# Combining two experts' outputs: a tile in two VectorE instructions, engines synchronised by hand

## The chip, the cores and the metric

The kernel runs on one core of a Trainium2 chip. The metric is the device time of one execution in microseconds; the kernel before takes 241.44 us (median of three runs, 241.16 to 241.47). The engines that matter here are VectorE (DVE in the profile), ScalarE (ACT), and SyncE (SP), which issues transfers; the transfers themselves run on the core's DMA engines. Slower, same or faster is judged at 2%.

## The reference

Each of 16 x 1024 tokens has two expert outputs of 512 values and two weights. The result is their weighted sum, all in float32:

```python
batch, seq, hidden, n_experts, k = 16, 1024, 512, 8, 2
# expert_outputs: (batch, seq, k, hidden), combine_weights: (batch, seq, k)
weights = combine_weights[..., np.newaxis]
return np.sum(expert_outputs * weights, axis=2).astype(np.float32)
```

So 67 MB are read and 33.6 MB are written, for three arithmetic operations per result.

## The kernel before

The 16,384 tokens are spread over 128 partitions, 128 tokens on each, and handled in 16 tiles of 8 tokens per partition (J = 8). A tile's load is 4 MB, its store 2 MB. There are four input and four output buffers. The framework places all waits between engines.

```python
wt = wpool.tile([P, per * k], dt)
for t, c in ((0, main), (main, J)):
    nc.scalar.dma_start(            # weights: 120 KB for tiles 0-14, then 8 KB for the last
        out=wt[:, k * t : k * (t + c)].rearrange("p (t k) -> p t k", k=k), in_=cw(t, c))

for g in range(per // J):
    et = ipool.tile([P, J, k * h], dt)       # 4 buffers
    ot = opool.tile([P, J, h], dt)           # 4 buffers
    nc.sync.dma_start(out=et, in_=eo(g * J, J))
    c0 = 0
    for c in (2, 2, 2, 2) if g == last else (J,):
        for i in range(c0, c0 + c):
            # ... w0, w1: this token's two weights, one value per partition
            if t == 0 or g == last:
                nc.scalar.activation(out=ot[:, i, :], in_=et[:, i, 0:h], func=copy, scale=w0)
            else:
                nc.vector.tensor_scalar_mul(out=ot[:, i, :], in0=et[:, i, 0:h], scalar1=w0)
            nc.vector.scalar_tensor_tensor(
                out=ot[:, i, :], in0=et[:, i, h : 2 * h], scalar=w1,
                in1=ot[:, i, :], op0=mult, op1=add)
        (nc.sync if g == last else nc.scalar).dma_start(
            out=o(g * J + c0, c), in_=ot[:, c0 : c0 + c, :])
        c0 += c
```

A tile is thus 16 VectorE instructions over 512 elements per partition: eight products and eight multiply-and-adds. ScalarE makes the first product of the first token and those of the last tile.

Of the kernel before, what the change touches and what calls it, by code (L numbers as in the profile page):

```python
# [1 line left out]

# [4 lines left out]


@with_exitstack
def kernel(  # L10
    ctx: ExitStack,
    tc: tile.TileContext,
    expert_outputs: bass.AP,
    combine_weights: bass.AP,
    out: bass.AP,
):

    nc = tc.nc  # L20
    b, s, k, h = expert_outputs.shape
    assert k == 2
    n = b * s
    P = nc.NUM_PARTITIONS
    per = n // P
    assert per * P == n
    J = 8
    main = per - J
    eo = expert_outputs.rearrange("b s k h -> (b s) (k h)")
    cw = combine_weights.rearrange("b s k -> (b s) k")  # L30
    o = out.rearrange("b s h -> (b s) h")

    def rows(x):

        a = x[0 : P * main, :].rearrange("(p t) f -> p t f", p=P)
        b = x[P * main : n, :].rearrange("(p t) f -> p t f", p=P)
        return lambda t, c: a[:, t : t + c, :] if t < main else b[:, t - main : t - main + c, :]

    eo, cw, o = rows(eo), rows(cw), rows(o)

    dt = mybir.dt.float32
    mult = mybir.AluOpType.mult
    add = mybir.AluOpType.add
    copy = mybir.ActivationFunctionType.Copy

    last = per // J - 1

    wpool = ctx.enter_context(tc.tile_pool(name="w", bufs=1))
    ipool = ctx.enter_context(tc.tile_pool(name="in", bufs=4))
    opool = ctx.enter_context(tc.tile_pool(name="out", bufs=4))  # L50

    wt = wpool.tile([P, per * k], dt)
    for t, c in ((0, main), (main, J)):
        nc.scalar.dma_start(
            out=wt[:, k * t : k * (t + c)].rearrange("p (t k) -> p t k", k=k), in_=cw(t, c)
        )

    for g in range(per // J):
        et = ipool.tile([P, J, k * h], dt)
        ot = opool.tile([P, J, h], dt)  # L60
        nc.sync.dma_start(out=et, in_=eo(g * J, J))  # L61
        c0 = 0
        for c in (2, 2, 2, 2) if g == last else (J,):
            for i in range(c0, c0 + c):
                t = g * J + i
                w0, w1 = wt[:, 2 * t : 2 * t + 1], wt[:, 2 * t + 1 : 2 * t + 2]


                if t == 0 or g == last:
                    nc.scalar.activation(out=ot[:, i, :], in_=et[:, i, 0:h], func=copy, scale=w0)  # L70
                else:
                    nc.vector.tensor_scalar_mul(out=ot[:, i, :], in0=et[:, i, 0:h], scalar1=w0)  # L72
                nc.vector.scalar_tensor_tensor(  # L73
                    out=ot[:, i, :],
                    in0=et[:, i, h : 2 * h],
                    scalar=w1,
                    in1=ot[:, i, :],
                    op0=mult,
                    op1=add,
                )  # L80

            (nc.sync if g == last else nc.scalar).dma_start(  # L82
                out=o(g * J + c0, c), in_=ot[:, c0 : c0 + c, :]
            )
            c0 += c


# [1 line left out]
_INS = ['expert_outputs', 'combine_weights']  # L89
_OUTS = [((16, 1024, 512), 'float32')]  # L90


# [23 lines left out]
```

## Time and profile before

| What | Value |
|---|---|
| time, median | 241.44 us |
| span of the profiled execution | 239.5 us |
| VectorE busy | 133.3 us, 247 instructions |
| ScalarE busy | 7.0 us, 10 instructions |
| bytes moved | 100.81 MB |
| a tile's load, issue to landing (median) | 49.5 us |
| a tile's store, issue to landing (median) | 24.1 us |

The page of the profile begins with the busy time of each engine. Below it the span is cut into 40 slices of 6 us: a digit is the busy share of a slice in tenths, and the row GB/s is what the DMA engines moved. Then come the DMA queues, the chain of work that ended last, the costliest groups of instructions (source line, engine, operation, output and inputs with their shapes, count; busy time and mean ns of one; idle time before them and what ended it), and the DMA issues (size of each, median time from issue to landing). Line 61 of the kernel is the load, 82 the stores, 72 and 73 the two VectorE instructions, 70 the ScalarE product, 54 the weights.

### The profile page before, as it was taken

Reading aid. Unit: us, or ns where it says so; the run is one execution under the profiler, and the core shown is the slowest. Engines: PE = TensorE matmul, PEld = TensorE weight load, DVE = VectorE, ACT = ScalarE, POOL = GpSimd, SP = SyncE. Lnnn points to the kernel's source line nnn. Section 1 sums busy time; section 2 is a strip of 40 time slices with the busy share of each in tenths; the row PEclk is TensorE's granted clock in tenths of the full one; section 3 lists DMA queues with packets and bytes.
Section 4 is the critical chain, followed back from the end, with each engine's and each line's share of the span. In section 5 each row is a group of like instructions: output and inputs, shape, how many; then the busy total and the mean of one; then the engine's idle time right before and its main releaser. Section 6 shows DMA issues by size and latency. Waiting matters only on the chain.

```text
span 239.5 us, 382 instructions
## 1 busy us (share of the span) xinstructions
DVE 133.3 (56%) x247; ACT 7.0 (3%) x10; POOL 0.2 (0%) x4
## 2 busy tenths in 40 slices
DVE  0077928529185490945819277291852918549080
ACT  0030000000000000000000000000000000000080
POOL 0000000000000000000000000000000000000000
DMA  7999899999999999999999999999999999999995
GB/s 268 451 441 439 350 438 476 401 432 424 411 441 435 479 394 438 435 441 400 435 438 441 435 460 413 438 402 432 437 435 479 397 438 427 449 397 435 438 409 213
DMA packets 5330, 100.81 MB, mean 421 GB/s; under 512 B 720, under 2 KB 848, under 8 KB 1360
## 3 DMA queue, kind: packets, MB, share of 16 engines
q1 hardware_dynamic: 2880, 69.21, 67.6%
q10 hardware_dynamic: 2448, 31.59, 30.9%
q14 instruction: 2, 0.02, 0.0%
HBM read 67.24 MB, written 33.55 MB: 421 GB/s over the span
## 4 chain that ended last, share of the span: by engine, by line
DMA 56%; DVE 26%; another core or an unknown queue 13%; issue 1%; SPq 0%; ACT 0%; DVEq 0%; ACTq 0%
DMA et<-in_expert_outputs_dram 56%; DVE ot L73 17%; DVE ot L72 10%; SPq L61 0%; ACT ot L70 0%; DVEq L111 0%; ACTq L82 0%; DVEq L72 0%; ACTq L70 0%
## 5 line engine op out<-in xcount | busy, mean ns | idle before, releaser
L72 DVE TENSOR_SCALAR ot<-et,wt 128x512 f32<-128x512 f32 x119 | 52.3, 481 | 93.7 <-DMA et<-in_expert_outputs_dram 80.2
L73 DVE SCALAR_TENSOR_TENSOR ot<-et,wt,ot 128x512 f32<-128x512 f32 x128 | 89.8, 745 | 6.7 <-ACT ot L70 6.7
L70 ACT ACTIVATE ot<-et,wt 128x512 f32<-128x512 f32 x9 | 5.7, 709 | 212.2 <-DMA et<-in_expert_outputs_dram 212.2
L70 ACT ACT_TABLE_LOAD x1 | 1.3, 1283 | 13.4 <-DMA et<-in_expert_outputs_dram 13.4
L100 POOL MEMSET const-bfloat16-1.0<- 128x1 bf16 x1 | 0.1, 102 | 0.0
L100 POOL MEMSET const-uint8-127<- 128x1 uint8 x1 | 0.1, 102 | 0.0
L100 POOL MEMSET const-float32-0.0<- 128x1 f32 x1 | 0.1, 99 | 0.2 <-issue 0.2
L100 POOL MEMSET const-float32-1.0<- 128x1 f32 x1 | 0.1, 99 | 0.0
## 6 DMA issues: line engine op xcount, KB each, us to landing
et<-in_expert_outputs_dram SPq DMA_DIRECT2D x16, 4096.0 KB, 49.5
out_dram<-ot ACTq DMA_DIRECT2D x15, 2048.0 KB, 24.1
out_dram<-ot SPq DMA_DIRECT2D x4, 512.0 KB, 4.9
wt<-in_combine_weights_dram ACTq DMA_DIRECT2D x1, 120.0 KB, 12.8
wt<-in_combine_weights_dram ACTq DMA_DIRECT2D x1, 8.0 KB, 22.1
```

Source lines behind the costliest of these rows:

```text
L70: nc.scalar.activation(out=ot[:, i, :], in_=et[:, i, 0:h], func=copy, scale=w0)
L72: nc.vector.tensor_scalar_mul(out=ot[:, i, :], in0=et[:, i, 0:h], scalar1=w0)
L73: nc.vector.scalar_tensor_tensor(out=ot[:, i, :], in0=et[:, i, h : 2 * h], scalar=w1, in1=ot[:, i, :], op0=mult, op1=add,)
L100: nc = _bacc.Bacc("TRN2", target_bir_lowering=False, num_devices=1)
```

## The change

Two things change. A tile other than the last becomes two VectorE instructions: one product of the whole 8 x 2 x 512 elements with the weights, broadcast along the last dimension, in place in the input buffer; and one sum of the two halves into the output buffer. And the whole kernel lies in one critical section with semaphores set by hand: one for each load, one for each output buffer's stores, and counters for VectorE and ScalarE. The aim is fewer instructions and fewer waits. Where the waits stand changes too: SyncE waits for the store of tile g-4 before it issues the load of tile g, so that VectorE needs to wait for the load alone; VectorE waits once for both transfers of weights; ScalarE runs a one-element activation before it issues the weights. The last tile keeps its form.

```diff
+    loaded = [nc.alloc_semaphore(f"loaded{g}") for g in range(G)]
+    stored = [nc.alloc_semaphore(f"stored{i}") for i in range(NOUT)]
+    # ... weights, tail, vec, act
+    made = [2 * (g + 1) for g in range(G - 1)]
+    with tc.tile_critical():
+        for g in range(G):
+            if g >= NOUT:
+                nc.sync.wait_ge(stored[g % NOUT], 16 * (g // NOUT))
+            ins = nc.sync.dma_start(out=et[:, g % NIN], in_=eo(g * J, J).rearrange("p j (k h) -> p j k h", k=k))
+            if g >= NIN:
+                ins._wait_ge(vec, made[g - NIN])
+            ins.then_inc(loaded[g], 16)
+
+        nc.scalar.activation(out=warm, in_=one, func=copy)
+        for t, c in ((0, main), (main, J)):
+            nc.scalar.dma_start(out=wt[:, t : t + c], in_=cw(t, c)).then_inc(weights, 16)
+        for g in range(G - 1):
+            nc.scalar.dma_start(out=o(g * J, J), in_=ot[:, g % NOUT])._wait_ge(
+                vec, made[g]
+            ).then_inc(stored[g % NOUT], 16)
+
+        nc.vector.wait_ge(weights, 32)
+        for g in range(G - 1):
+            ek = et[:, g % NIN].rearrange("p j k h -> p (j k) h")
+            wb = wt[:, g * J : (g + 1) * J].rearrange("p j k -> p (j k)").unsqueeze(2)
+            nc.vector.tensor_tensor(
+                out=ek, in0=ek, in1=wb.to_broadcast([P, J * k, h]), op=mult
+            )._wait_ge(loaded[g], 16).then_inc(vec, 1)
+            e = et[:, g % NIN]
+            nc.vector.tensor_tensor(
+                out=ot[:, g % NOUT], in0=e[:, :, 0], in1=e[:, :, 1], op=add
+            )._wait_ge(vec, made[g] - 1).then_inc(vec, 1)
+        # ... the last tile: ScalarE's eight products, VectorE's eight multiply-and-adds,
+        # ... stores of two tokens each by SyncE; then SyncE waits for all stores
-            for i in range(c0, c0 + c):
-                # ... the pairs of instructions per token, shown above
```

More of the change, by code (lines that the diff above doesn't have):

```diff
@@ L27 @@
     J = 8
+    NIN = NOUT = 4
+    G = per // J
     main = per - J
-    eo = expert_outputs.rearrange("b s k h -> (b s) (k h)")
-    cw = combine_weights.rearrange("b s k -> (b s) k")
-    o = out.rearrange("b s h -> (b s) h")
     def rows(x):
@@ L37, in rows @@
         return lambda t, c: a[:, t : t + c, :] if t < main else b[:, t - main : t - main + c, :]
-    eo, cw, o = rows(eo), rows(cw), rows(o)
+    eo = rows(expert_outputs.rearrange("b s k h -> (b s) (k h)"))
+    cw = rows(combine_weights.rearrange("b s k -> (b s) k"))
+    o = rows(out.rearrange("b s h -> (b s) h"))
     dt = mybir.dt.float32
@@ L44 @@
     copy = mybir.ActivationFunctionType.Copy
[L46 to L63, printed above, removed]
-            for i in range(c0, c0 + c):
[L65 to L85, printed above, removed]
@@ new lines @@
+    pool = ctx.enter_context(tc.tile_pool(name="sbuf", bufs=1))
+    wt = pool.tile([P, per, k], dt)
+    warm = pool.tile([P, 1], dt)
+    et = pool.tile([P, NIN, J, k, h], dt)
+    ot = pool.tile([P, NOUT, J, h], dt)
+    loaded = [nc.alloc_semaphore(f"loaded{g}") for g in range(G)]
+    stored = [nc.alloc_semaphore(f"stored{i}") for i in range(NOUT)]
+    weights = nc.alloc_semaphore("weights")
+    tail = nc.alloc_semaphore("tail")
+    vec = nc.alloc_semaphore("vec")
+    act = nc.alloc_semaphore("act")
@@ new lines @@
+    one = nc.const_aps.tensor(1.0, (P, 1), dt)
+    PIECE = 2
+    made = [2 * (g + 1) for g in range(G - 1)]
[25 more added lines that the diff above has]
+            )._wait_ge(vec, made[g] - 1).then_inc(vec, 1)
+        g = G - 1
+        nc.scalar.wait_ge(weights, 32)
+        for i in range(J):
+            e, r = et[:, g % NIN, i], ot[:, g % NOUT, i]
+            w = wt[:, g * J + i]
+            ins = nc.scalar.activation(out=e[:, 0], in_=e[:, 0], func=copy, scale=w[:, 0:1])
+            if i == 0:
+                ins._wait_ge(loaded[g], 16)
+            ins.then_inc(act, 1)
+            nc.vector.scalar_tensor_tensor(
+                out=r, in0=e[:, 1], scalar=w[:, 1:2], in1=e[:, 0], op0=mult, op1=add
+            )._wait_ge(act, i + 1).then_inc(vec, 1)
+            if i % PIECE == PIECE - 1:
+                f = i + 1 - PIECE
+                nc.sync.dma_start(
+                    out=o(g * J + f, PIECE), in_=ot[:, g % NOUT, f : i + 1]
+                )._wait_ge(vec, made[g - 1] + i + 1).then_inc(tail, 16)
+        for i in range(NOUT):
+            nc.sync.wait_ge(stored[i], 16 * len(range(i, G - 1, NOUT)))
+        nc.sync.wait_ge(tail, 16 * (J // PIECE))
```

## The prediction, made before the change was run

> **What bounds the kernel now.** I read the page from the top. First the two sections on the span and the transfers:
>
> ```profile
> span 239.5 us, 382 instructions
> ...
> DVE 133.3 (56%) x247; ACT 7.0 (3%) x10; POOL 0.2 (0%) x4
> ...
> DMA  7999899999999999999999999999999999999995
> GB/s 268 451 441 439 350 438 476 401 432 424 411 441 435 479 394 438 435 441 400 435 438 441 435 460 413 438 402 432 437 435 479 397 438 427 449 397 435 438 409 213
> ...
> HBM read 67.24 MB, written 33.55 MB: 421 GB/s over the span
> ```
>
> VectorE (DVE) works 56% of the span; the row DMA reads 9 in almost every slice except the first and last. The kernel is a copy machine: 100.8 MB at some 430 GB/s are 234 us, and only about 5 us of head and tail are not transfer. So nothing that VectorE saves can shorten the span much; a change can only add idle DMA time, or shave the 5 us.
>
> The chain that ended last, in order of time, says the same, two stretches of it shown:
>
> ```profile
> 60.76 49.49 DMA et<-in_expert_outputs_dram
> 110.25 0.03 issue
> ...
> 118.92 49.44 DMA et<-in_expert_outputs_dram
> 168.36 0.03 issue
> ```
>
> A load issued at 60.76 lands 49.5 us later, because three older loads are queued in front of it: the load queue is never empty. From 110.25 to 168.36 four tiles pass: 58.1 / 4 = **14.5 us per tile**, the DMA's pace. Then the groups and the DMA issues:
>
> ```profile
> L72 DVE TENSOR_SCALAR ot<-et,wt 128x512 f32<-128x512 f32 x119 | 52.3, 481 | 93.7 <-DMA et<-in_expert_outputs_dram 80.2
> L73 DVE SCALAR_TENSOR_TENSOR ot<-et,wt,ot 128x512 f32<-128x512 f32 x128 | 89.8, 745 | 6.7 <-ACT ot L70 6.7
> L70 ACT ACT_TABLE_LOAD x1 | 1.3, 1283 | 13.4 <-DMA et<-in_expert_outputs_dram 13.4
> ...
> out_dram<-ot ACTq DMA_DIRECT2D x15, 2048.0 KB, 24.1
> ...
> wt<-in_combine_weights_dram ACTq DMA_DIRECT2D x1, 120.0 KB, 12.8
> wt<-in_combine_weights_dram ACTq DMA_DIRECT2D x1, 8.0 KB, 22.1
> ```
>
> VectorE idles 80 us for loads. The last line matters most for the change: the second weights transfer, 8 KB, takes **22.1 us** to land. Before, only the last tile reads it.
>
> [...]
> - [...] the first transfer lands with tile 0 (12.8 us against 12.6 for the first load) and the second with tile 1 (22.1 against 21.9).
> - [...] 481 ns for the one-tensor product and 745 ns for the two-tensor operation over 512 elements.
> - [...]
>
> **The change part by part.**
>
> *VectorE's work.* Before, a tile is 8 pairs; in the chain two products take 0.79 and two sums 1.32 us, so 4 x 2.11 = 8.5 us. After, one product over 8 x 2 x 512 = 8192 elements and one sum over 4096, both two-tensor fp32, [...] I take **13.25 us, up by 4.7 per tile**: fewer instructions, [...]. It is still under the 14.5 us of the DMA, so in the steady state all of it is hidden: cost 0. If it exceeded 14.5, the excess would count 15 times.
>
> *Weights.* VectorE now waits for both weights transfers before its first tile, and ScalarE issues them only after a warm-up activation with its table load: [...]. Two or so load packets later than before's 23.3, so the first product starts at about **25 us instead of 13.5**.
>
> *The load gate.* SP now waits before load g for the store of tile g-4 to have landed, where before it waited for VectorE only. This takes a store's time to landing out of the slack of four input buffers: loads queue two or three deep instead of four. In the steady state the loop of four tiles has 4 x 14.5 = 58 us; load 15, VectorE 13, store 20 to 24 are within that, so the load queue still never empties: cost 0.
>
> *The start, where the two meet.* Sizes: a load alone takes 21.9 - 12.6 = 9.3 to 9.8 us (with its later issue 9.8), a store of half the bytes 4.9. From the packet and landing records I read about 1.5 us between a transfer's last byte, its landing, the next issue and that one's first byte.
> - Loads 0 to 3 land at 13.3, 23.1, 32.9, 42.7 with no store between them.
> - VectorE ends tiles 0, 1, 2, 3, 4 at 25 + 13.25 n: 38, 51.5, 65, 78, 91.
> - Store 0 goes at 38, shares with load 3, and all queued bytes are gone at about 42.3 + 4.9 = 47. Only then may load 4 go: **gap 1, 1.5 us**; it moves from 48.5.
> - Load 4 and store 1 (from 51.5) are 14.7 us of work: done at 63. Load 5 waits for store 1: **gap 2, 1.5 us**.
> - Load 5 and store 2, from 64.7 to 79.4: **gap 3, 0 to 1.5 us**, as store 3 (78) begins to fill it.
> - Store 3 is away before load 6 ends, so load 7 is queued in time; from about 95 us loads overlap again and no gap is left.
> Sum 3 to 4.5 us; lost DMA time can't be won back, since the DMA is the bound for the rest. I take **4 us**.
>
> *Tail.* The last tile stays as it was: eight ScalarE products, eight VectorE sums, four stores by SP. Tile 14 lands near 213 or 214 (before 213.0), VectorE ends it 13 us later, near 227, as load 15 lands (before 227.5): 0. *Synchronisation by hand* replaces waits that lay beside the transfers: 0 to -0.5 us, and the block's entry could cost as much.
>
> Total: 241.44 + 4 = **245.4 us**.
>
> **Rivals.**
> - *Nothing happens, 241 to 242 us.* The DMA bound hides all. For it: 14.5 against 13.25 us, and four buffers. If the store gate had slack from the start (stores landing in 7 us while loads still queue), or the weights came at 14 us as before, the gaps vanish. Against it: no load beyond the fourth can be issued before the first store has landed, near 47 us, and the first four are over at 43.
> - *VectorE becomes the bound, 250 to 265 us.* If a tile took 15 us, 25 + 15 x 15 + last tile and tail 17 would be 267. For it: the margin is only 1.3 us of 14.5, and the product is in place with a broadcast operand, which no row here shows. [...] At 14 us the start alone would cost some 9 us.
> - *The latencies are longer under load:* a store takes 24.1 us to land in the queue, and the final 512 KB stores 4.9 us where their bytes need 1.2. With 2.5 to 3 us per gap, 7 to 8 us: 249.
> - *A gain:* the head and tail hold 5 us, most of it first-byte and landing latency that stays. Under 1 us.
>
> **Range and chances.** The gaps put the centre at +4 (+1.7%), just under the limit of 2% (246.3). The DMA can't do better than now by more than a microsecond, and the first rival sets the low end at 241.5; the latencies and a late table load set the high end at 249.5. Same is likeliest (0.60), slower by over 2% has 0.38, faster 0.02.
>
> **What would show it.** The product at about 8.7 us and the sum at 4.4; the first product at about 25 us, released by the weights; VectorE busy near 200 us (15 x 13.1 + 5; over 80%); SP waiting for stores rather than for VectorE; the DMA row with lower digits only between 40 and 95 us and 9s after; time from issue to landing of loads down from 49 to some 20 to 35 us. Wrong if the product takes over 9.5 us (VectorE bound), if the weights land by 15 us, if the early slices stay at 9, or if gaps recur through the whole span.

## The result, and the profile after

The changed kernel takes **244.84 us** (median of five runs, 244.49 to 245.22) against 241.3: a ratio of 1.0148, interval 1.0134 to 1.0162. It is slower by 3.5 us, inside the 2% that count as the same. The prediction said 245.4 us, 241.5 to 249.5.

The page of the changed kernel, first the span, the engines and the two rows of 40 slices (6.1 us each):

```profile
span 243.2 us, 153 instructions
...
DVE 201.4 (83%) x38; ACT 6.5 (3%) x10; POOL 0.2 (0%) x4
...
DMA  7999999789999999999999999999999999999996
GB/s 264 444 434 432 431 431 377 313 299 458 396 469 437 393 434 412 426 415 431 415 437 442 426 431 412 431 455 412 431 450 431 447 437 410 458 431 399 431 415 280
...
L90 DVE TENSOR_TENSOR et<-et,wt 128x8192 f32<-128x8192 f32 x15 | 130.3, 8688 | 31.7 <-DMA wt<-in_combine_weights_dram 23.5
L94 DVE TENSOR_TENSOR ot<-et 128x4096 f32<-128x4096 f32 x15 | 66.4, 4425 | 0.5
...
et<-in_expert_outputs_dram SPq DMA_DIRECT2D x16, 4096.0 KB, 21.8
```

VectorE went from 247 instructions to 38 and from 133.3 to 201.4 us of work. That alone costs nothing, as experiment 2 below shows (240.39 us with a product of 8.69 us). What costs is three slices of the row GB/s, the seventh to the ninth (377, 313, 299 GB/s, 36 to 55 us): apart from the first and last slices, which both kernels have, this is the one place where the transfers slacken. The windows of that stretch (start and end, length, busy time of VectorE, ScalarE and GpSimd, clock, DMA share, GB/s) narrow it down:

```profile
30.00:40.00 10.00, 9.97 (x3) 0.00 (x0) 0.00 (x0) 1.00 1.01 426
40.00:45.00 5.00, 5.00 (x1) 0.00 (x0) 0.00 (x0) 1.00 0.86 318
45.00:50.00 5.00, 4.96 (x3) 0.00 (x0) 0.00 (x0) 1.00 0.84 305
50.00:55.00 5.00, 5.00 (x1) 0.00 (x0) 0.00 (x0) 1.00 0.78 292
55.00:60.00 5.00, 4.96 (x2) 0.00 (x0) 0.00 (x0) 1.00 0.99 423
```

These views count a packet, one piece of a transfer on one DMA engine, where it starts. If packets are instead cut at the ends of a window, each DMA engine is idle for 2.0 us between 45 and 50 us and for next to nothing in the two windows beside it; there GB/s is low because load packets took longer than usual (1.81 and 1.45 us on average for those that began from 40 to 45 and from 50 to 55 us, against 1.213 between 110 and 228 us).

The waits of SyncE's queue (us in all, times, longest) name the releaser. The largest row before (line 61 is the load), then after (line 70 is the wait ahead of a load):

```profile
SPq L61 <- DVE ot L73: 113.3, 12, 18.9
```

```profile
SPq L70 <- DMA out_dram<-ot: 200.5, 12, 45.5
```

Before, the loads waited for VectorE. After, twelve loads, all after the fourth, waited for a store, the longest 45.5 us. The packet records of the trace give the order of events: the first four loads are over at 43.6 us; store 0, issued at 36.7, lands at 48.5; only then does the fifth load (load 4, counted from 0 as in the code) go out, at 48.6, and its first packet moves at 49.5. Store 1 is issued at 49.7, too late to fill the hole. From 48.1 to 49.5 nothing moves at all.

Summed over the 16 DMA engines, the packet records account for the difference. "Long packets" is what load packets of 32 KB took beyond their usual 1.213 us; the small packets of the weights, under 1 KB, count as idle time, some 0.4 us in both kernels:

| us per DMA engine | before | after | difference |
|---|---|---|---|
| idle, first packet to the last load's end | 0.6 | 2.6 | +2.0 |
| long packets | 1.4 | 3.9 | +2.5 |
| idle after the last load | 1.5 | 0.4 | -1.2 |
| first packet to last packet | 236.4 | 239.7 | +3.3 |

The other 0.4 us of the span lies ahead of the first and behind the last packet. So there are two losses in the first 110 us, and a small gain at the end that the prediction had not seen.

### The profile page after: what moved, and what is told of

It is laid out like the page before. It is cut to its first block, busy times and chain, and to the rows that moved or that the text cites. A ratio compares the mean times of both kernels' runs of the same rounds, so it can differ in the third digit from the quotient of the medians.

```text
span 243.2 us, 153 instructions
## 1 busy us (share of the span) xinstructions
DVE 201.4 (83%) x38; ACT 6.5 (3%) x10; POOL 0.2 (0%) x4
## 4 chain that ended last, share of the span: by engine, by line
DVE 51%; DMA 45%; ACT 0%; issue 0%; SPq 0%; ACTq 0%; DVEq 0%
DVE et L90 32%; DMA out_dram<-ot 18%; DMA et<-in_expert_outputs_dram 18%; DVE ot L94 16%; DMA wt<-in_combine_weights_dram 9%; DVE ot L109 2%; ACT et L105 0%; ACT L77 0%; SPq L70 0%; ACTq L145 0%; DVEq L86 0%; SPq L65 0%
## 5 line engine op out<-in xcount | busy, mean ns | idle before, releaser
L90 DVE TENSOR_TENSOR et<-et,wt 128x8192 f32<-128x8192 f32 x15 | 130.3, 8688 | 31.7 <-DMA wt<-in_combine_weights_dram 23.5
L94 DVE TENSOR_TENSOR ot<-et 128x4096 f32<-128x4096 f32 x15 | 66.4, 4425 | 0.5
L105 ACT ACTIVATE et<-et,wt 128x512 f32<-128x512 f32 x8 | 5.0, 710 | 227.3 <-DMA et<-in_expert_outputs_dram 227.3
L109 DVE SCALAR_TENSOR_TENSOR ot<-et,wt 128x512 f32<-128x512 f32 x8 | 5.4, 746 | 2.1 <-ACT et L105 2.1
```

Of the source, the lines that this page charges most:

```text
L90: nc.vector.tensor_tensor(out=ek, in0=ek, in1=wb.to_broadcast([P, J * k, h]), op=mult)._wait_ge(loaded[g], 16).then_inc(vec, 1)
L94: nc.vector.tensor_tensor(out=ot[:, g % NOUT], in0=e[:, :, 0], in1=e[:, :, 1], op=add)._wait_ge(vec, made[g] - 1).then_inc(vec, 1)
L105: ins = nc.scalar.activation(out=e[:, 0], in_=e[:, 0], func=copy, scale=w[:, 0:1])
L109: nc.vector.scalar_tensor_tensor(out=r, in0=e[:, 1], scalar=w[:, 1:2], in1=e[:, 0], op0=mult, op1=add)._wait_ge(act, i + 1).then_inc(vec, 1)
```

## The experiments

The theory: three things together make the loss, namely the late first product (both weights awaited), the slow tile (13.1 us), and the gate (load g waits for store g-4). Any one taken away should close the gap. The rivals: the section synchronised by hand costs by itself; or one or two of the three are enough. The numbers in the table are those of the experiments below; "kernel 3" is the kernel of experiment 3.

| kernel | gate on loads | VectorE starts | tile | time, us | ratio to before, interval |
|---|---|---|---|---|---|
| changed | yes | 23.5 | 13.1 | 244.84 | 1.0148 (1.0134 to 1.0162) |
| 1. gate on VectorE | no | 23.5 | 13.1 | 240.87 | 0.9983 (0.9976 to 0.9989) |
| 2. first weights only | yes | 13.7 | 13.1 | 240.39 | 0.9961 (0.9949 to 0.9974) |
| 3. pairs by hand | yes | 23.5 | 8.5 | 241.65 | 1.0014 (1.0008 to 1.0021) |
| 4. padded | yes | 23.5 | 14.0 | 248.30 | 1.0290 (1.0274 to 1.0306) |
| 5. padded, gate on VectorE | no | 23.6 | 14.0 | 248.36 | 1.0291 (1.0277 to 1.0305) |
| 6. padded, first weights | yes | 14.0 | 14.0 | 240.69 | 0.9976 (0.9967 to 0.9985) |
| 7. both waits moved | no | 13.7 | 13.1 | 240.51 | 0.9966 (0.9953 to 0.9978) |
| 8. last four in pairs | yes | 13.8 | 13.1 / 8.5 | 240.94 | 0.9986 (0.9980 to 0.9993) |

**1. The gate on VectorE.** The wait for a store moves from the load to the sum that overwrites the output buffer (and likewise for the last tile).

```diff
-            if g >= NOUT:
-                nc.sync.wait_ge(stored[g % NOUT], 16 * (g // NOUT))
...
             e = et[:, g % NIN]
+            if g >= NOUT:
+                nc.vector.wait_ge(stored[g % NOUT], 16 * (g // NOUT))
             nc.vector.tensor_tensor(out=ot[:, g % NOUT], ..., op=add)
```

> The changed kernel with one wait moved: VectorE's sum waits for the output buffer's store, SyncE waits only for VectorE before the next load. Theory (gate, late weights and slower tile together open gaps in the DMA between 40 and 100 us): the fifth load no longer waits for the first store, the DMA row reads 9 from the second slice to the last but one, and the time goes back to 241 to 242 us. First rival (the section synchronised by hand costs the 3.5 us whatever its waits): 244 to 245. Second rival (the 13 us tile and the late first product are enough by themselves): 244 to 245, with the early slices still low.

It took 240.87 us, a little under what was expected. The page's VectorE row and DMA row:

```profile
DVE  0000999999999999999999999999999999997800
...
DMA  7999999899999999999999999999999999999996
```

The 7 and the 8 have shrunk to one 8. Load 4 is issued at 36.7 us, as soon as VectorE is through with its buffer. Both rivals that the expectation named fall: the section is as before but for one wait, VectorE starts as late and works as slowly, and the 3.5 us are gone. VectorE now runs from 23.5 us to the last tile without a pause and ends tile 14 at 219.5 us, just as load 15 lands, so it is close to being the bound.

**2. The first weights only.** Each weights transfer gets its own semaphore; VectorE starts on the first.

```diff
-        nc.vector.wait_ge(weights, 32)
+        nc.vector.wait_ge(weights[0], 16)
...
         g = G - 1
+        nc.vector.wait_ge(weights[1], 16)
```

> The changed kernel with one other wait moved: VectorE starts after the first transfer of weights, only the last tile waits for the second; the gate on the loads stays. Theory: the first product starts near 13.5 us, the first store is issued near 26.5 us and lands before the fourth load's bytes are done, so that no gap opens: 241 to 242 us. If the gate is enough by itself (rival): 243.5 to 245. If hand synchronisation costs (rival): 244 to 245.

It took 240.39 us, below the low end of what was expected, and 0.4% below the kernel before. The groups and the DMA row:

```profile
DMA  7999999999999999999999999999999999999996
...
L90 DVE TENSOR_TENSOR et<-et,wt 128x8192 f32<-128x8192 f32 x15 | 130.3, 8690 | 26.7 <-DMA wt<-in_combine_weights_dram 13.7
```

VectorE starts ten us earlier (13.7 against 23.5), with the gate in place and the slow tile, and the low digits are gone. Store 0 lands at 45.7 us, so load 4 goes out before load 3 has ended (48.4), and store 1 moves from 46.1. So the gate and the slow tile together do no harm.

**3. Pairs by hand.** The old sixteen instructions per tile inside the changed kernel's section; gate and late start kept.

```diff
-            nc.vector.tensor_tensor(out=ek, in0=ek, in1=wb.to_broadcast([P, J * k, h]), op=mult)
-            nc.vector.tensor_tensor(out=ot[:, g % NOUT], in0=e[:, :, 0], in1=e[:, :, 1], op=add)
+            # for each pair of tokens: two tensor_scalar_mul into ot,
+            # then two scalar_tensor_tensor, each waiting for its product
```

> The changed kernel with the old form of a tile: eight one-tensor products and eight multiply-and-adds per tile, order and shapes as before, in the hand-synchronised section, with the gate on the loads and the wait for both weights kept. Theory: a tile takes 8.5 instead of 13.1 us, the first store goes at 32 instead of 36.7 us and the next ones 8.5 us apart, so the gaps close: 241 to 242 us. Rival (hand synchronisation or the gate alone costs): 244 to 245.

It took 241.65 us, as expected. A fast tile makes up for the late start, but not quite as expected: load 4 still goes out late, at 48.0 us, and its first packet moves at 52.0. The hole is filled by store 1, which was issued at 40.6 and moves from 47.2 to 52.9. Hand synchronisation, gate and late start with the old arithmetic come to +0.14%; what hand synchronisation alone does is not separated here.

In experiments 1 to 3 the long packets are back at 1.4 to 1.6 us per engine, as before (1.4); in the changed kernel they were 3.9. So they come and go with the gap. Each experiment leaves two of the three conditions in place, so no one and no two of them make the loss.

**4. The padded tile.** One more addition of 840 elements per tile, whose result is not used.

```diff
+            nc.vector.tensor_tensor(
+                out=pad, in0=e[:, 0:2, 0, 0:420], in1=e[:, 0:2, 1, 0:420], op=add
+            )._wait_ge(vec, made[g] - 1)
```

> The changed kernel with one more VectorE addition of 840 elements per tile into a scratch tile that nothing reads, about 0.9 us, so 14.0 instead of 13.1 us per tile. It stays under the DMA's 14.5 us. Theory: the late start leaves VectorE 23.5 + 15 x 14.0 = 233.5 us for tile 14, later than the last load's landing near 229, so VectorE now sets the end: 248 to 251 us. Rival (a VectorE tile under 14.5 us is hidden beside the DMA): 244.5 to 246.

It took 248.30 us: 0.95 us more per tile cost 3.5 us more in all, though the tile at 14.0 is still under the DMA's 14.5. The end of the chain shows why (start, length, what):

```profile
219.67 8.61 DVE et L91
228.28 0.02 issue
228.31 1.03 DVE pad L95
229.34 4.35 DVE ot L98
...
234.16 0.73 ACT et L109
234.91 5.39 DVE ot L113 x8
```

It is VectorE from the first product to the last tile: 23.5 + 15 x 14.0 = 233.5 (measured 233.7), and the last tile follows. By then load 15 has been there for 2 us (231.6): VectorE's total, with its late start, has become longer than that of the loads.

**5 and 6. The padded tile with the gate on VectorE, and with the first weights.** The edits of 1 and 2 applied to 4.

> The padded tile (14.1 us by the profile of the padded run) with the gate moved from SyncE to VectorE. Theory: with this tile it is no longer the gate that costs; VectorE runs without a pause from 23.5 us and ends tile 14 at 23.5 + 15 x 14.1 = 235, so the time stays at 247.5 to 249 us although the loads come early. Rival (the gate's gaps make up the 7 us of the padded run): 241 to 244.

> The padded tile with the gate kept and VectorE started by the first weights. Theory: VectorE starts ten us earlier and could end tile 14 at 13.7 + 15 x 14.1 = 225, before the last load lands, so the slower tile is hidden: 240.3 to 242 us. Rival (a tile of 14 us costs by itself beside the DMA's 14.5): 244 to 249.

They took 248.36 and 240.69 us. With the 14.0 us tile, taking the gate away brings nothing, while the earlier start brings all of it. The wait ahead of the last tile's first product (line, releaser; us in all, times, longest) tells the two bounds apart, first with the gate on VectorE, then with the first weights:

```profile
ACT et L109 <- DVE ot L97: 231.9, 1, 231.9
```

```profile
ACT et L110 <- DMA et<-in_expert_outputs_dram: 222.5, 1, 222.5
```

In the first, the last tile's products begin when VectorE has ended tile 14 (233.8 us); its load had landed at 218.5. In the second they begin when the load lands, at 224.8 us; VectorE had ended tile 14 only 0.4 us earlier.

**7. Both waits moved.** The edits of 1 and 2 together.

> Both waits moved: gate on VectorE and start by the first weights. Theory: either one alone closes the gaps, so the second brings nothing more: 240.2 to 241.3 us. If the two costs add up (rival), this is about 1 us below the better of the two single moves, under 239.7.

It took 240.51 us, as expected and the same as with the first weights only. The costs do not add up; they are conditions of one loss.

**8. Fast tiles at the end.** Kernel 2 with tiles 11 to 14 in pairs.

```diff
+    FAST = 4
...
+            if g >= G - 1 - FAST:   # tiles 11 to 14: the pairs of kernel 3
```

> The version with the first weights only, where tiles 11 to 14 have the old form of eight products and eight multiply-and-adds (8.5 us), the rest as it is. Theory of the end: in the version with the first weights only the slow tile leaves more store work for the time after the last load, 13.0 us of it against 11.7 before, and this hides the last tile's compute; with fast tiles at the end the stores go earlier, less is left, and the DMA idles about a microsecond before the last stores: 241.0 to 241.7 us. Rival (the 0.9 us below the kernel before come from hand synchronisation or fewer instructions): 240.3 to 240.6.

It took 240.94 us, just under the theory's range (241.0 to 241.7) and above the rival's (240.3 to 240.6). By the packet records the DMA idles after the last load for 0.3 us in kernel 2, 0.8 here, 1.4 with pairs throughout (kernel 3) and 1.5 in the kernel before, and has 12.8, 12.1, 9.7 and 10.1 us of transfers left at that point; the times are 240.39, 240.94, 241.65 and 241.29. This fits the theory of the end: slow tiles hold stores back, and these are then left to move while the last tile is computed. Idle time makes 1.1 of the 1.3 us between kernels 2 and 3. Between kernel 2 and the kernel before, the idle time differs by 1.2 us, and kernel 2 moves nothing for 0.4 us longer ahead of its first and behind its last packet; the two make up the 0.9 us, within 0.1. That the slow tiles are the cause of all of that idle time is not shown: four fast tiles brought back about half of it.

Kernels 2 and 7 are the fastest here, 0.4% and 0.3% below the kernel before. In kernel 2 the DMA is idle for under a microsecond between its first and last packet, so there is little left to gain for this amount of data.

## Why the prediction was right, point by point

- **VectorE's work** held: about 8.7 and 4.4 us were the author's estimates, which the profile before did not show (it has a two-tensor operation in one size alone, 745 ns for 512 elements); 8.688 and 4.425 us were measured. The two together take 13.07 us from tile to tile, not the 13.25 that the author estimated: a product begins a little before the preceding sum has ended (the second product at 36.56 us, the first sum's end at 36.64).
- **The rates**: fewer instructions, more work. An element of the product took 0.94 ns before (481 ns for 512) and 1.06 after (8688 for 8192). The products went from 52 us to 130, over twice as many elements, since before the second expert's products lay in the multiply-and-adds.
- **Weights** held in the main: the first product starts at 23.5 us, released by the weights (25 predicted). The second transfer took 22.0 us to land (22.1 before): its 128 packets of 64 bytes, 11 ns each, moved from 13.7 to 22.8 us, spread among the 128 packets of the second load (12.5 to 22.8). The step that failed is the delay by the warm-up activation: the weights were issued at 0.96 us, while the table load ran from 0.90. ScalarE's queue did not wait for it:

```profile
0.90 1.28 ACT L77 ACT_TABLE_LOAD   x1 [0.90 <-SPq L65]
...
0.96 0.88 ACTq L79 DMA_DIRECT2D wt<-in_combine_weights_dram  x2
```

- **The load gate costs nothing in the steady state** held: between 110 and 228 us the packet records show under 0.05 us of idle time per engine. In experiments 2 and 6, with the gate, no gap opens at the start either.
- **The gaps** held in kind and in sum, not in number. Predicted were two or three of 1.5 us each; there was one true gap, the first, put at 47 to 48.5 and measured from 48.1 to 49.5 us (2.0 us of idle time per engine, as not all engines ran dry at once). The second was filled: VectorE had started 1.5 us earlier than predicted and its tile was shorter, so store 2 went out at 62.8 us (65 predicted) and store 1 and then store 2 kept the engines busy until load 5 moved. The step on load 7 failed: it was to be queued in time, but waited for store 3 until 95.7 us, when load 6 had ended (95.3); store 4 filled that hole. The gap cost more than the round trip, as packets after the restart were long: 1.2 us more in the same stretch, 0.7 where load 7 restarts, at 95 to 110 us, and 0.5 in smaller parts. With 2.0 us idle and 1.2 of long packets that gap cost about 3, the size that the rival of longer latencies gave a gap (2.5 to 3), but there was only one.
- **The tail** was put at 0 and gained about 1.2 us of idle time. The mis-sized terms: +4.5 for the start instead of +4, -1.2 for the end, and +0.4 ahead of the first and behind the last packet, where the prediction gave hand synchronisation -0.5 to 0, or a like cost. They partly cancelled, so it is partly luck that the number came within 0.6 us.
- **The rival that VectorE becomes the bound** was nearer than its numbers said. The prediction set its tile of 13.25 against 14.5 us and put some 9 us on a tile of 14 us; experiments 4 and 5 measured 7, and show that the sum of all tiles after the late start makes them, not the gaps.

## What to carry to other kernels

When a transfer-bound kernel gives an engine more work, don't compare its tile with the transfers' tile alone: add the time at which it starts, and ask how early the first buffers come free. A wait moved to where it is easy to write (a load that waits for a store, a start that waits for data only the last tile needs) was harmless here while queues were full (under 0.05 us of idle time per engine from 110 to 228 us), and opened a gap where they were still filling (nothing moved from 48.1 to 49.5 us). Three harmless things can make one loss; take each away alone before you blame one.

## What was not expected of the hardware

In the changed kernel a transfer that joined while the other queue was at work started late: load 5 was issued at 66.3 us and its first packet moved at 70.2, load 7 at 95.7 and 99.5, store 1 at 49.7 and 54.3; load 4, on idle engines, started 1.0 us after its issue. And the packets of load 4, the first after the gap, took 1.375 us on average and up to 2.1, against 1.213 in the steady state. Those of load 5 and load 7, which restarted beside a store, took 1.247 and 1.304. No run here shows why.
